# A one-core encoder layer with MoE: one gather over all 512 slots, another split of slot sizes, and where a bias, a scale and a PSUM bank come from

## The chip, the cores and the metric

The kernel runs on one NeuronCore of a Trainium2 chip. The metric is the device time of one execution in microseconds (us), as a median of several. TensorE (PE) multiplies, VectorE (DVE), ScalarE (ACT) and GpSimd (POOL) do the rest of the arithmetic, and SyncE (SP) issues nearly all loads from HBM, in the order in which they are written.

## What is computed

One layer over 256 tokens of 2048 channels, batch 1. A vector c gives six modulation vectors, `mod = SiLU(c) @ W_ada + b_ada`: shift, scale and gate for the mixer and for the FFN. What the change touches is this skeleton of the reference:

```python
h = rms_norm(x, g_mix) * (1 + sc1) + sh1
x = x + g1 * (token_mixer(h, w_in, ...) @ w_out)
h = rms_norm(x, g_ffn) * (1 + sc2) + sh2
x = x + g2 * moe_ffn(h)        # 16 experts, every token goes to two of them
# moe_ffn: for each expert e, its rows xb of h (512 rows in all):
#   hid = silu(xb @ w_gate[e]) * (xb @ w_up[e]);   y = hid @ w_down[e]
```

Everything is float32. With the reference's own inputs the router sends 77, 70, 62, 59, 56, 33, 30, 27, 26, 16, 15, 14, 12, 11, 4 and 0 rows to the experts, sorted by load.

## The kernel before

The program is written in the order in which each engine runs it; engines meet only at semaphores.

**Mixer (0 to about 355 us).** `h` is made in five chunks of channels (`make_h`): for each 128 channels, a matmul of `xa` (x, tokens on the partitions) with `diag`, a diagonal matrix of 1/rms, transposes and scales x at once into a PSUM bank (L409); DVE applies the modulation and `split` writes a hi and a lo part in fp32r. Weights of w_in are split the same way, hi by ACT (L175), lo by DVE or POOL (L176), and three matmuls (`mm3`: hi*hi, lo*hi, hi*lo) make one product of nearly float32 accuracy. `pm()` deals three PSUM banks in turn. Tiles of w_ada run between the pieces: `ada_parts` multiplies on PE into one of two banks `accs`, each with a matmul for the bias at its end (L270); `sum_parts` does it on DVE.

**w_out (about 355 to 470 us).** Four column blocks n, each with two pm banks and 16 weight pieces; `x1_block` on DVE, POOL and ACT adds the result to xa. DVE also sums w_ada for g1 here. Tiles of w_ada for g2 start in block 3 and go on through the routing.

**Routing (470 to 532 us).** Router logits give a 0/1 matrix M (L1001). PE, in its queue after g2 tiles, counts and ranks (L1007 to L1012, into `pp`); DVE sorts the experts by load (`key`, `irow`, `pos`) and builds `oneh` (L1085 to L1087): for each of 512 slots a one in the row of the token that fills it, times its 1/rms. `gather` multiplies xa by oneh in plain float32, first for slots 0 to 255 into pm banks, then, just ahead of the experts, for slots 256 to 511 (L1343), and writes `XT`, the experts' input. `irow` holds the experts' numbers; SP needs it before it can load an expert.

**Experts (532 to 1440 us).** `CAPS` gives the slots per rank: the three busiest get 128, six get 64, six get 32, the last none. `ORDER` mixes the ranks in time. An expert is 12 tiles of 2 MB (8 for gate and up, 4 for down) through a ring of six wide buffers (`wide`): four from the earlier ring, and two (`ringl`) that are laid where the mixer's tiles were. For 128 slots the weights are split and every product is three matmuls; for 64 and 32 it is one plain float32 matmul on a part of the array. An expert whose rows exceed its slots gets a pass of 128 slots in a loop at the end (L1362), which runs as often as a count computed on the chip.

Of the kernel before, what the change touches and what calls it, by code (L numbers as in the profile page):

```python
# [43 lines left out]
CAPS = [128] * 3 + [64] * 6 + [32] * 6 + [0]  # L44
# [72 lines left out]
def body(tc, x_d, prm_d, bg_d, wada_d, win_d, wout_d, egu_d, ed_d, out_d):  # L117
# [107 lines left out]
    psM, s_psM = pool("psM", 3, space=PSUM)  # L225
# [7 lines left out]
    lgp = lgp[:, 0:256]  # L233
    def pm():
        return psM.tile([128, 512], F32, name="pm")
# [19 lines left out]
    def ada_parts(sec, k0, nk, after, acc, bias=None):  # L255
# [4 lines left out]
        def one(g):  # L260
# [139 lines left out]

    def make_h(q):
# [291 lines left out]
    mod2.extend((f, None) for f in steps(ada_parts(2, 0, 4, lambda P: g1_first.append(P), 1, 0)))  # L693
# [18 lines left out]
    for q in range(last):  # L712
# [93 lines left out]
    rt, s_rt = pool("rt")  # L806

# [14 lines left out]
    G.iota(ec, pattern=[[1, 1]], base=0, channel_multiplier=1, allow_small_or_imprecise_dtypes=True)  # L822
    revc = rtile([16, 1], "revc")
# [4 lines left out]
    o = 0  # L828
# [73 lines left out]
    def g1_steps(n):  # L902
        r4s.append(grow())
        if n == 0:
            S.copy(r4s[0], g1_first[0])
# [3 lines left out]
        return steps(sum_parts(2, 4 * n, 4, lambda a: None, n % 2, ENG(G1[n]), lambda: r4s[n], n))  # L909
# [10 lines left out]

    r2, g2p, g1s = [], deque(), {}
# [37 lines left out]

    B3 = [128, 2, 16]  # L960
# [10 lines left out]
    V.reciprocal(sc, sc)  # L971
    sl = rtile(B3, "sl")
# [68 lines left out]
    V.tensor_copy(irow[:, 0:16], po[0:1, 0:16])  # L1041
    order = rtile([128, 16], "order")
# [15 lines left out]
    s_py.close()  # L1058
    s_hp.close()
    s_pb.close()  # L1060
    s_c1.close()
    pg2, s_pg2 = pool("pg2", 1, side="right")
    g2w = pg2.tile([128, D], F32, name="g2w")
    wides += [pg2.tile([128, 2 * RINGW], F32, name=f"ringl{i}") for i in range(RING_LAST)]
    old = wides[:RING + RING_MORE]
    used = [max(i for i, x in enumerate(ring_tiles) if x is a or x is b) for a, b in halves_of]
    wide_ring = deque(wides[RING + RING_MORE:] + [t for _, t in sorted(zip(used, old), key=lambda x: x[0])])

    def wide():
        wide_ring.rotate(-1)  # L1070
        return wide_ring[-1]

    XT = pg2.tile([128, KD, 512], F32, name="XT")

# [350 lines left out]
```

## Time and profile before

| | us |
|---|---|
| median of 3 runs (lowest to highest) | 1436.28 (1435.34 to 1439.57) |
| the profiled execution's own time | 1442.07 |
| its span in the trace | 1440.2 |
| busy: PE / DVE / ACT / POOL | 1247.2 / 693.2 / 417.1 / 160.5 |
| read from HBM | 535.85 MB |

A busy PE is not one at its peak: a matmul's row lasts from its start to its modelled end, and rows overlap. The stretches are best read by two things, the GB/s of the loads and what PE waits for. Times in the rows are us from the start of the span.

### The profile page before, as it was taken

The numbers are of one execution on the slowest core, as the hardware profiler recorded it, in microseconds if no ns is written. First come the engines' busy times: TensorE is split into PE (matmuls) and PEld (weight loads), VectorE is DVE, ScalarE is ACT, GpSimd is POOL, SyncE is SP. The second block draws the span as 40 slices with busy tenths as digits, with TensorE's granted clock in tenths as the row PEclk, the third lists the DMA queues.
The fourth block names the chain that finished last, engine by engine and source line by source line (L and its number), as shares of the span: only waits on it lengthen the run. The fifth ranks groups of instructions, "written<-read, shape, count | busy, mean of one in ns | idle before, by whom it ended". The sixth has DMA issues, their size and how long they took to land.

```text
span 1440.2 us, 17629 instructions
## 1 busy us (share of the span) xinstructions
PE 1247.2 (87%) x6844; PEld 683.4 (47%) x6844; DVE 693.2 (48%) x1271; ACT 417.1 (29%) x754; POOL 160.5 (11%) x127
## 2 busy tenths in 40 slices
PE   5998999998999896999969999689997889858876
PEld 3665776664776372764326743257533222222221
DVE  4466675755795643893228842269611211202112
ACT  4532334445343140771006820048300000000000
POOL 1333332312443000000000000000000000000000
PEclk9999999999999898999989999899999999989988
DMA  9979696889888579998999989999899999999997
GB/s 391 377 312 348 237 375 227 313 334 352 355 301 344 212 296 428 427 415 339 427 426 426 424 315 428 428 425 427 308 420 426 425 427 427 426 427 426 427 427 296
DMA packets 49209, 539.15 MB, mean 374 GB/s; under 512 B 5464, under 2 KB 5592, under 8 KB 7008
## 3 DMA queue, kind: packets, MB, share of 16 engines
q1 hardware_dynamic: 47664, 534.79, 90.7%
q10 hardware_dynamic: 1456, 3.17, 0.6%
q8 instruction: 55, 0.90, 0.3%
q14 instruction: 34, 0.28, 0.1%
HBM read 535.85 MB, written 2.10 MB: 374 GB/s over the span
## 4 chain that ended last, share of the span: by engine, by line
PE 59%; DMA 26%; DVE 7%; issue 3%; ACT 2%; POOL 1%; SPq 0%; DVEq 0%; ACTq 0%; POOLq 0%
PE lbank L171 29%; PE pm L171 18%; DMA ring<-in_e_down_dram 11%; DMA ringl<-in_e_gu_dram 7%; DMA ring<-in_e_gu_dram 7%; PE bank L171 6%; PE ada L171 4%; PE pt L171 1%; DVE ada L294 1%; DMA ring<-in_w_ada_dram 1%; DVE whl L176 1%; DVE el L176 1%; ACT whl L175 1%; DVE z L451 1%; POOL whl L176 0%
## 5 line engine op out<-in xcount | busy, mean ns | idle before, releaser
L171 PE MATMUL pm<-whl,hT 128*128 128x512 f32 x1120 | 296.6, 400 | 9.7 <-DVE whl L176 3.9
L171 PEld LDWEIGHTS pm<-whl,hT 128*128 128x128 f32 x1120 | 208.8, 190 | 82.9 <-issue 12.8
L171 PE MATMUL lbank<-ringl,xr 128*32 128x256 f32 (+1 forms) x1152 | 143.1, 494 | 38.1 <-DMA ringl<-in_e_gu_dram 37.8
L171 PE MATMUL lbank<-el,xs 128*128 128x512 f32 x576 | 138.3, 398 | 9.5 <-ACT el L175 6.5
L176 POOL TENSOR_TENSOR whl<-ring,whl 128x512 fp32r<-128x512 f32 x86 | 120.0, 1407 | 225.4 <-ACT whl L175 201.9
L171 PE MATMUL lbank<-ring,xr 128*32 128x256 f32 (+1 forms) x864 | 104.3, 484 | 34.8 <-DMA ring<-in_e_gu_dram 34.7
L171 PEld LDWEIGHTS lbank<-el,xs 128*128 128x128 f32 x576 | 108.1, 190 | 39.9 <-ACT el L175 9.7
L175 ACT CAST whl<-ring 128x512 fp32r<-128x512 f32 x172 | 99.9, 622 | 72.6 <-PE pm L171 62.5
L171 PE MATMUL bank<-y,gt 128*128 128x512 f32 x240 | 118.0, 614 | 0.0
L1304 DVE TENSOR_TENSOR xa<-xa,bank 128x512 f32<-128x512 f32 x120 | 82.5, 688 | 68.5 <-PE bank L171 68.5
L171 PE MATMUL lbank<-ring,hidT 128*64 128x512 f32 (+1 forms) x576 | 104.6, 630 | 10.9 <-DMA ring<-in_e_down_dram 10.9
L171 PEld LDWEIGHTS lbank<-ringl,xr 128*32 128x32 f32 (+1 forms) x1152 | 52.0, 127 | 129.1 <-issue 68.0
L1295 DVE TENSOR_TENSOR y<-lbank,g2w 128x512 f32<-128x512 f32 x60 | 41.5, 692 | 147.9 <-PE lbank L171 147.9
L176 DVE TENSOR_TENSOR whl<-ring,whl 128x512 fp32r<-128x512 f32 x86 | 83.9, 991 | 38.0 <-ACT whl L175 37.7
L175 ACT CAST el<-ring 128x512 fp32r<-128x512 f32 x144 | 90.0, 625 | 29.3 <-PE lbank L171 21.6
L176 DVE TENSOR_TENSOR el<-ring,el 128x512 fp32r<-128x512 f32 x144 | 92.7, 689 | 0.0
L1191 ACT COPY gt<-bank 128x256 f32<-128x256 f32 x15 | 5.6, 373 | 290.0 <-PE bank L1189 290.0
L1245 DVE TENSOR_TENSOR hid<-hid,lbank 128x512 f32<-128x512 f32 x12 | 8.3, 688 | 164.7 <-PE lbank L171 164.5
L171 PEld LDWEIGHTS lbank<-ring,xr 128*32 128x32 f32 (+1 forms) x864 | 39.1, 127 | 98.8 <-DMA ring<-in_e_gu_dram 48.9
L171 PE MATMUL ada<-ring,cact 128*1 128x512 f32 (+1 forms) x568 | 68.6, 585 | 19.7 <-DMA ring<-in_w_ada_dram 14.0
L171 PE MATMUL lbank<-el,hidT 128*128 128x512 f32 x288 | 74.9, 412 | 12.1 <-DVE el L176 8.3
L175 ACT CAST el<-ringl 128x512 fp32r<-128x512 f32 x96 | 58.7, 624 | 79.5 <-DMA ringl<-in_e_gu_dram 64.8
(377 smaller groups left out, 1185.4 us busy)
## 6 DMA issues: line engine op xcount, KB each, us to landing
ringl<-in_e_gu_dram SPq DMA_DIRECT2D x60, 2048.0 KB, 20.1
ring<-in_e_gu_dram SPq DMA_DIRECT2D x45, 2048.0 KB, 24.3
ring<-in_e_down_dram SPq DMA_DIRECT2D x45, 2048.0 KB, 25.7
ring<-in_w_ada_dram SPq DMA_DIRECT2D x79, 1024.0 KB, 7.1
ring<-in_w_in_dram SPq DMA_DIRECT2D x30, 1024.0 KB, 8.2
ringm<-in_e_gu_dram SPq DMA_DIRECT2D x15, 2048.0 KB, 21.0
ringm<-in_e_down_dram SPq DMA_DIRECT2D x15, 2048.0 KB, 21.5
ring<-in_w_out_dram SPq DMA_DIRECT2D x12, 1024.0 KB, 8.2
```

The costliest lines, as they stand in the source:

```text
L171: E.matmul(out, lhsT=lhsT, rhs=rhs, start=start, stop=stop, skip_group_check=True)
L175: S.copy(hi, src)
L176: (eng or V).tensor_tensor(lo, src, hi.bitcast(F32), op=OP.subtract)
L294: eng.scalar_tensor_tensor(P, w[:, j, :], ck, P, op0=OP.mult, op1=OP.add)
L451: V.tensor_tensor(dst, dst, P[h], op=OP.add)
L1191: S.copy(gt, p[:, :256])
L1245: V.tensor_tensor(hid[:, o], hid[:, o], P[2 * b + 1], op=OP.mult)
L1295: V.tensor_tensor(y, P, g2w[:, c0:c0 + 512], op=OP.mult)
L1304: V.tensor_tensor(a, a, p, op=OP.add)
```

## The change

- `CAPS` becomes two ranks of 128, seven of 64, six of 32.
- The three pm banks are now fixed tiles in a deque; when the last product with `accs[1]` is done (g1's first part), `accs[1]` joins them as a fourth. All w_ada products behind it use `accs[0]`.
- `ada_parts` loses its bias matmul. The rows of the bias come by eight small DMAs on ACT's queue into `bgr`, and `gate_row` adds one row on DVE behind ACT's copy. (The parts that DVE sums keep their bias.)
- `scaled` (ACT) writes x times 1/rms for a chunk into `xn`; `make_h` transposes it with the identity; `diag` is gone.
- The gather is one pass: `x_hi` (ACT) and `x_lo` (DVE) split x times 1/rms into fp32r, `oneh` holds plain ones, and each 128 channels take four fp32r matmuls of 512 columns; ACT writes all of XT. The second gather is gone.
- To make room, the mixer's pools close before the routing (`ones` and `stri` are copied), `xhl` and `oneh` lie where `ringl` was, and `ringl` follows them. The experts' ring now begins with the four older buffers.

```diff
-CAPS = [128] * 3 + [64] * 6 + [32] * 6 + [0]
+CAPS = [128] * 2 + [64] * 7 + [32] * 6 + [0]
...
+    pbanks = deque(psM.tile([128, 512], F32, name=f"pm{i}") for i in range(3))
     def pm():
-        return psM.tile([128, 512], F32, name="pm")
+        pbanks.rotate(-1)
+        return pbanks[-1]
...
-                if g == ng - 1 and bias is not None:
-                    mm(P[0:1, :], ident[0:8, bias:bias + 1], bgt, start=False)
...
+    def scaled(q):
+        k0, nk = CHUNKS[q]
+        for h in range(2):
+            S.activation(xn[:, h, :128 * nk], xa[:, h, 128 * k0:128 * k0 + 128 * nk], AF.Identity, scale=rsx[:, h:h + 1])
...
-                mm(p[:, 128 * h:128 * h + 128], xa[:, h, 128 * k:128 * k + 128], diag[:, h, :])
+                E.transpose(p[:, 128 * h:128 * h + 128], xn[:, h, 128 * c:128 * c + 128], ident)
...
+    def gate_row(sec, q, out, P):
+        S.copy(out, P)
+        o = slice(32 * q, 32 * q + 1)
+        V.tensor_tensor(out[o, :], out[o, :], bgr[o, sec // 3, :], op=OP.add)
...
+    for q in range(4):
+        for a in range(2):
+            nc.scalar.dma_start(bgr[32 * q:32 * q + 1, a, :], bg_d[a:a + 1, 512 * q:512 * q + 512])
...
+    g1_load(1)
+    pbanks.append(accs[1])
...
+    def x_hi():
+        for c, h in parts:
+            o = slice(1024 * c, 1024 * c + 1024)
+            S.activation(xhl[:, 0, h, o], xa[:, h, o], AF.Identity, scale=rs1[:, h:h + 1])
+
+    def x_lo(n):
+        for _ in range(n):
+            c, h = parts.pop(0)
+            o = slice(1024 * c, 1024 * c + 1024)
+            V.scalar_tensor_tensor(xhl[:, 1, h, o], xa[:, h, o], rs1[:, h:h + 1], xhl[:, 0, h, o].bitcast(F32),
+                                   op0=OP.mult, op1=OP.subtract)
...
     V.reciprocal(sc, sc)
+    x_hi()
...
-    mm(pp[:, 16:32], ones, M[:, 0, :], start=False)
+    mm(pp[:, 16:32], one2, M[:, 0, :], start=False)
+    x_lo(2)
...
     V.tensor_copy(irow[:, 0:16], po[0:1, 0:16])
+    x_lo(2)
...
-        V.tensor_scalar(oneh[:, h, :], io512, sl2[:, 0, h:h + 1], rs1[:, h:h + 1], op0=OP.is_equal, op1=OP.mult)
-        V.tensor_scalar(oht, io512, sl2[:, 1, h:h + 1], rs1[:, h:h + 1], op0=OP.is_equal, op1=OP.mult)
-        V.tensor_tensor(oneh[:, h, :], oneh[:, h, :], oht, op=OP.add)
+        V.tensor_scalar(oneh[:, h, :], io512, sl2[:, 0, h:h + 1], None, op0=OP.is_equal)
+        V.scalar_tensor_tensor(oneh[:, h, :], io512, sl2[:, 1, h:h + 1], oneh[:, h, :].bitcast(F32),
+                               op0=OP.is_equal, op1=OP.add)
...
+            for i in range(2):
+                mm(p, xhl[:, i, h, 128 * k:128 * k + 128], oneh[:, h, :], h + i == 0, h + i == 2)
+        S.activation(XT[:, k, :], p, AF.Identity, scale=mod[:, 3, k:k + 1], bias=mod[:, 2, k:k + 1])
...
+    s_phl.close()
+    pl, s_pl = pool("pl", 1, side="right")
+    wides += [pl.tile([128, 2 * RINGW], F32, name=f"ringl{i}") for i in range(RING_LAST)]
...
-    for k in range(KD):
-        gather(1, k, bank)
```

DVE in the routing, from M (which expert each token takes) to the copy of the ranks, `pos`. Before:

```order
L1001 TENSOR_TENSOR M<-oh_3680,oh_3687 128x32
L1029 SCALAR_TENSOR_TENSOR key<-pt_119,rev 128x16
L1030 SCALAR_TENSOR_TENSOR keyc<-pt_119,revc 16x1
L1032 TENSOR_SCALAR rkc<-key,keyc 16x16
L1033 TENSOR_REDUCE rkc<-rkc 16x1
L1035 TENSOR_SCALAR ohc<-ioE,rkc 16x16
L1041 CAST irow<-pt_120 1x16
L1043 COPY order<-pt_120 128x16
L1045 COPY pos<-pt_119 128x48
```

After, in the same place on DVE (`grow_3328` to `grow_3330` are the g2 rows of chunks 1 to 3, `xhl` is written by x_lo):

```order
L1050 TENSOR_TENSOR M<-oh_3608,oh_3615 128x32
L797 TENSOR_TENSOR grow_3328<-grow_3328,bgr 1x512
L797 TENSOR_TENSOR grow_3329<-grow_3329,bgr 1x512
L1004 SCALAR_TENSOR_TENSOR xhl<-xa,rs_3530,xhl 128x1024 x2
L1079 SCALAR_TENSOR_TENSOR key<-pt_122,rev 128x16
...
L1085 TENSOR_SCALAR ohc<-ioE,rkc 16x16
L797 TENSOR_TENSOR grow_3330<-grow_3330,bgr 1x512
L1091 CAST irow<-pt_123 1x16
L1004 SCALAR_TENSOR_TENSOR xhl<-xa,rs_3530,xhl 128x1024 x2
L1094 COPY order<-pt_123 128x16
L1096 COPY pos<-pt_122 128x48
```

Two row additions and two halves of x_lo now stand ahead of `key`, one addition ahead of `irow`, and two more halves of x_lo ahead of `order` and `pos`.

ACT in the same stretch, before, from the router's exponential to the first gather's writes:

```order
L346 ACTIVATE rs_3620<-rs_3620 128x2
L969 ACTIVATE sc<-sc 128x32
L789 COPY grow_3416<-ada_114 128x512
L789 COPY grow_3417<-ada_113 128x512
L789 COPY grow_3418<-ada_114 128x512
L1096 ACTIVATE XT<-pm,mod 128x256 x16
```

After:

```order
L346 ACTIVATE rs_3530<-rs_3530 128x2
L1017 ACTIVATE sc<-sc 128x32
L998 ACTIVATE xhl<-xa,rs_3530 128x1024 x4
L795 COPY grow_3328<-ada_113 128x512
L795 COPY grow_3329<-ada_113 128x512
L795 COPY grow_3330<-ada_113 128x512
L1127 ACTIVATE XT<-pm_120,mod 128x512
```

The four halves of x_hi stand ahead of the copy of g2's chunk 1, and all three copies now read the one bank ada_113 (`accs[0]`), where before they took turns with ada_114.

## Rows read from the trace of the kernel before

**Rows 1.** The page: GB/s in 40 equal slices of the span (36 us each)

```profile
GB/s 391 377 312 348 237 375 227 313 334 352 355 301 344 212 296 428 427 415 339 427 426 426 424 315 428 428 425 427 308 420 426 425 427 427 426 427 426 427 427 296
```

**Rows 2.** Windows (busy us of PE, PEld, DVE, ACT, POOL; clock; DMA share; GB/s)

```profile
1010.00:1050.00 40.00, 37.96 (x152) 20.51 (x154) 22.09 (x37) 12.88 (x21) 0.00 (x0) 1.00 0.83 317
1100.00:1400.00 300.00, 233.39 (x1342) 78.02 (x1346) 53.22 (x100) 4.43 (x10) 0.00 (x0) 0.94 1.01 427
```

**Rows 3.** The page's costliest groups: matmuls of the three 128-slot experts

```profile
L171 PE MATMUL lbank<-el,xs 128*128 128x512 f32 x576 | 138.3, 398 | 9.5 <-ACT el L175 6.5
...
L171 PE MATMUL lbank<-el,hidT 128*128 128x512 f32 x288 | 74.9, 412 | 12.1 <-DVE el L176 8.3
```

**Rows 4.** Timeline of the routing, 478 to 496 us (start us, us, engine, line, operation)

```profile
478.76 0.23 ACT L969 ACTIVATE sc<-sc 128x32 f32<-128x32 f32 x1 [2.25 <-DVE sc L968]
...
482.35 3.59 PE L171 MATMUL ada<-ring,cact 128*1 128x512 f32 x16
482.45 0.59 ACT L789 COPY grow<-ada 128x512 f32<-128x512 f32 x1 [3.46 <-PE ada L171]
...
487.85 1.01 PE L171 MATMUL ada<-bgt,ident 8*1 8x512 f32 x2
488.79 0.62 PE L171 MATMUL pt<-M,ones 128*128 128x16 f32 x4
...
490.40 0.17 DVE L1029 SCALAR_TENSOR_TENSOR key<-pt,rev 128x16 f32<-128x16 f32 x1 [5.61 <-PE pt L171]
...
491.71 3.61 PE L171 MATMUL ada<-ring,cact 128*1 128x512 f32 x32
491.99 0.18 DVE L1045 COPY pos<-pt 128x48 f32<-128x48 f32 x1
...
495.70 0.54 DVE L1085 TENSOR_SCALAR ring<-io,sl,rs 128x512 f32<-128x512 f32 x1
```

**Rows 5.** The chain that ended last: an early w_in piece, then both gathers

```profile
67.58 5.68 PE pm L171 x24
...
499.12 18.77 PE pm L171 x70
517.89 14.31 PE bank L171 x64
```

**Rows 6.** First expert loads on SP's queue, and a window of the second gather

```profile
496.39 0.89 SPq L1312 DMA_DIRECT2D ringl<-in_e_gu_dram  x2
...
524.00:532.00 8.00, 8.00 (x37) 6.05 (x36) 2.72 (x5) 2.27 (x4) 0.00 (x0) 1.00 0.00 2
```

**Rows 7.** Waits of 345 to 478 us (total, times, longest), and a bias matmul

```profile
PE pm L171 <- DVE xg L855: 3.7, 3, 1.8
...
462.84 1.01 PE L171 MATMUL ada<-bgt,ident 8*1 8x512 f32 x2
```

**Rows 8.** Start of the w_out stage, and ACT's own DMAs (issue ns, landing us)

```profile
360.92 2.96 DVE L176 TENSOR_TENSOR whl<-ring,whl 128x512 fp32r<-128x512 f32 x3
...
L1273 ACTq DMA_DIRECT2D out_dram<-xa x8: 338/338/353, 1423.1 to 1434.1; - x8
...
DMA to landing us min/median/max: 2.7/3.1/5.2
```

**Rows 9.** Operations on ACT and DVE by shape (count | busy us, mean ns)

```profile
L375 ACT ACTIVATE hT<-xa 128x2048 fp32r<-128x2048 f32 x2 | 3.8, 1902 | 0.3 <-DMA xa<-in_x_dram 0.3
...
L175 ACT CAST whl<-ring 128x512 fp32r<-128x512 f32 x42 | 24.2, 621 | 18.1 <-PE pm L171 18.1
...
L294 DVE SCALAR_TENSOR_TENSOR ada<-ring,cact,ada 128x512 f32<-128x512 f32 x33 | 24.9, 754 | 1.0
```

**Rows 10.** Transposes by matmul, the DVE step behind one, and a window

```profile
L171 PE MATMUL pt<-diag,xa x60: 274/275/487, 21.6 to 228.0; 128*128 128x128 f32 x60
...
226.98 0.54 DVE L411 TENSOR_SCALAR hf<-pt,mod 128x256 f32<-128x256 f32 x1
...
220.00:240.00 20.00, 18.52 (x100) 12.74 (x101) 12.33 (x25) 7.82 (x15) 6.01 (x4) 1.00 0.34 124
```

More of the change, by code (lines that the diff above doesn't have):

```diff
@@ L266, in run @@
                     k, t = r * g + j, j % 4
-                    mm(P[32 * t:32 * t + 1, :128 * nk], cact[:, k:k + 1], w[:, j, :], start=k < 4,
-                       stop=k >= KD - 4 and (t > 0 or bias is None))
-                if g == ng - 1 and bias is not None:
-                    mm(P[0:1, :], ident[0:8, bias:bias + 1], bgt, start=False)
+                    mm(P[32 * t:32 * t + 1, :128 * nk], cact[:, k:k + 1], w[:, j, :], start=k < 4, stop=k >= KD - 4)
                 if g == ng - 1:
@@ L516, in body @@
         f()
+    scaled(0)
     flush()
@@ L692, in body @@
     g1_first = []
-    mod2.extend((f, None) for f in steps(ada_parts(2, 0, 4, lambda P: g1_first.append(P), 1, 0)))
+    mod2.extend((f, None) for f in steps(ada_parts(2, 0, 4, lambda P: g1_first.append(P), 1)))
     for i in range(4, 33, 4):
@@ L720, in body @@
                 piece(q, PIECES[i])
+            if i == 1:
+                then(lambda q=q: scaled(q + 1))
             for c in PLAN[q][i]:
@@ L822, in body @@
     G.iota(ec, pattern=[[1, 1]], base=0, channel_multiplier=1, allow_small_or_imprecise_dtypes=True)
+    one2 = rtile([128, 128], "one2")
+    V.tensor_copy(one2, ones)
+    stri2 = rtile([128, 128], "stri2")
+    V.tensor_copy(stri2, stri)
     revc = rtile([16, 1], "revc")
@@ L904, in g1_steps @@
         if n == 0:
-            S.copy(r4s[0], g1_first[0])
+            gate_row(2, 0, r4s[0], g1_first[0])
             return []
@@ L957, in body @@
     logit_b(3)
+    s_py.close()
+    s_hp.close()
+    s_pb.close()
+    s_c1.close()
+    pg2, s_pg2 = pool("pg2", 1, side="right")
+    g2w = pg2.tile([128, D], F32, name="g2w")
+    XT = pg2.tile([128, KD, 512], F32, name="XT")
+    phl, s_phl = pool("phl", 1, side="right")
+    xhl = phl.tile([128, 2, 2, D], F32R, name="xhl")
+    oneh = phl.tile([128, 2, 512], F32R, name="oneh")
+    parts = [(c, h) for c in range(2) for h in range(2)]
+    def x_hi():
[8 more added lines that the diff above has]
+                                   op0=OP.mult, op1=OP.subtract)
     B3 = [128, 2, 16]
@@ L1055, in body @@
     pick(start, tmp, cnt)
[L1058 to L1073, printed above, removed]
-    oneh = wide_ring[-1][:, :1024].rearrange("p (h s) -> p h s", h=2)
     sl1 = rtile(B3, "sl1")
@@ L1105, in body @@
     for k in range(KD):
-        gather(0, k, pm)
+        gather(k)
     cntR = rtile([128, 16], "cntR")
@@ L1161, in body, with wide @@
         S.copy(g2w[:, 512 * b:512 * b + 512], p)
+    s_phl.close()
+    pl, s_pl = pool("pl", 1, side="right")
+    wides += [pl.tile([128, 2 * RINGW], F32, name=f"ringl{i}") for i in range(RING_LAST)]
+    old = wides[:RING + RING_MORE]
+    used = [max(i for i, x in enumerate(ring_tiles) if x is a or x is b) for a, b in halves_of]
+    wide_ring = deque([t for _, t in sorted(zip(used, old), key=lambda x: x[0])] + wides[RING + RING_MORE:])
+    def wide():
+        wide_ring.rotate(-1)
+        return wide_ring[-1]
     s_rt.close()
```

37 lines of the change are left out of this document (15 added, 22 removed).

## The prediction

> **What bounds the kernel now.** I read the page's slices first, then windows where they dip, then the timeline of the routing, and last waits and single operations. The slices [rows 1] split the span in two. From slice 15 (540 us) on, the loads run at 424 to 428 GB/s but for three dips (slices 17 and 18, 23, 28) and the end; over 1100 to 1400 us it is 427 GB/s at a DMA share of 1.01, while PE is busy 233 of 300 us [rows 2]. So the experts are bound by their loads: a tile of 2.097 MB takes 4.91 us, and 180 tiles are needed. The dips lie in the three 128-slot experts, the only ones that split their weights; there PE is the bound and the ring is full. Before slice 13 the loads run mostly well under 427 GB/s: the mixer and w_out are bound by PE, with DVE close behind it in w_out. Between the two lies the routing, a chain of small DVE and PE steps and then the gathers, and in it the loads stand still: 2 GB/s in 524 to 532 us [rows 6], because the five free ring buffers are full and the experts have not begun.
>
> The end is therefore set by three things: when PE reaches the routing, when the loads run freely again, and how long they are held up later.
>
> **The change part by part.** The sum is made against the profiled execution's 1442.07 us, which is 5.8 us above the median of 1436.28; I take the same difference off both.
>
> 1. *The third 128-slot expert becomes a 64-slot one.* Its dip, 1010 to 1050 us, ran at 317 GB/s [rows 2]: 40 x (1 - 317/427) = 10.3 us of loading lost. Nothing in 1100 to 1400 us, where only 64 and 32 slots run, shows such a loss, so PE is late nowhere there and the whole of it should come back: **-10.3** (bounds -10.5 and -8). What is late next is the loads themselves.
>
> 2. *The gather and its chain.* Both gathers together run from 499.12 to 532.2 us, the second one alone 14.3 us for 64 instructions [rows 5]. The new gather is 64 fp32r instructions of 512 columns; such instructions run at 5.68/24 = 0.237 us each [rows 5], so 15.2 us. Saving 14 us of PE time is the easy part. The chain ahead of it grows, as the order of DVE and ACT shows:
>  - x_hi on ACT: 2048 columns took 1.902 us, 512 took 0.621 [rows 9], so 1024 about 1.05, and four 4.2. They start behind the exponential (478.99) [rows 4] and end near 483.2; only then comes the copy of g2's chunk 1 (0.59), which before ran at 482.45 [rows 4]. As all chunks now share one bank, PE starts chunk 2 near 484.0, where before it started at 482.35, in spite of the bias matmul that is gone. Its 32 instructions took 5.5 us to 487.85 [rows 4]. The counts (`pp`) stand behind them on PE: 489.5 for 488.79.
>  - DVE must then wait for ACT's copy of chunk 2 (done near 490.2), add a row of 512 (a DVE operation on 512 columns takes 0.754 [rows 9]; I take 0.7) and do two halves of x_lo. One is 1024 columns: between 0.754 and 1.51 (two of 512); I take 1.2. So `key` comes at 493.3, before at 490.40 [rows 4].
>  - `ohc` and its matmul come 1.4 us later, at 494.7. In before `irow` and `pos` followed at once, beside 32 instructions for chunk 3 (3.61 us) [rows 4]. Now DVE's addition for chunk 3 stands ahead of `irow`, so DVE waits for those: 3.6 us at the pace of rows 4, 6.9 if PE is as slow as at 482.35 (16 in 3.59); I take 4.5. With copy and addition that is 500.6; two more halves of x_lo: `pos` is done near 503.4, against 492.2: **11.2 us later**.
>  - From there `oneh` began 3.5 us later [rows 4], now near 506.9; four operations instead of six, 2.4 us: 509.3.
>  - The gather: 62 x 0.237 = 14.7, and some 1.6 us for a start at a low clock (the first gather's 62 last instructions took about 15.2 us, ahead of the g2w matmuls, at 0.224 each they would take 13.9). It ends near **525.6**, where the second gather ended at 532.2: 6.6 us earlier.
>  The loads: in before five tiles lay ready at 532.2 and the sixth could go; now four buffers can be filled early and the two `ringl` wait for the gather's end. One tile of 4.91 us fewer is ready 6.6 us earlier: **-1.7**. When the first tile is issued (496.39 [rows 6], now perhaps 501) no longer matters, since four take 20 us and are there before the gather ends. Bounds: x_lo at 0.75 each, PE at full pace and an x_hi that hides would bring 7 us more; all slow, and with a colder gather, 6 us less: -8 to +5.
>
> 3. *Fourth bank in w_out.* PE waited there for DVE to empty a bank, 3.7 us in three waits [rows 7]; with four banks the next block starts at once. DVE is busy nearly all the time there, so some of it may come back as a wait for split weights. I take **-2.5** (0 to -3.7).
>
> 4. *Bias matmuls.* A pair holds PE for about 0.95 us (487.85 to 488.79) [rows 4]. Those of g2's chunks 1 to 3 are in part 2, g1's lies beside ACT and DVE work. Chunk 0's, inside PE-bound w_out, counts: **-0.95**.
>
> 5. *Transposes of scaled x.* 16 times, four instructions (two float32 matmuls make 64; 60 of them read as 275 ns, mostly latency [rows 10]) become two. But a chunk's modulation on DVE, 0.54 us each [rows 10], and the hi and lo behind it set the pace, five times. I take 0.2 us per chunk of the five: **-1.0** (0 to -3). The scaling by ACT is ten operations of 256 or 512 columns, hidden, since ACT has a piece's time to spare; with no cover it would be under 6 us.
>
> 6. *Eight small DMAs on ACT's queue at the start of w_out.* Each costs ACT some 0.34 us of issue (eight stores took 338 to 353 ns) and lands 2.7 to 5.2 us later [rows 8]. They stand ahead of the first weight splits, and DVE's first row addition waits for them, ahead of its first lo part, which began at 360.92 [rows 8] and which PE waited for. Issue of eight (2.7 us) and the last one's landing make 5.4 to 7.9 us behind ACT's last mixer step; part of it is covered by DVE's own set-up steps ahead of 360.92, the addition (0.7) is not. **+1.5** (0.7 to 4). The Trainium skill, "DMA: Bandwidth & Descriptors", section "Anatomy of one DMA", gives a small DMA about 2.0 us in all; no row here has one so small, and by it this term would be near +0.7.
>
> Sum: -10.3 - 1.7 - 2.5 - 0.95 - 1.0 + 1.5 = **-15 us**: 1427 for the profiled execution, **1421 us** for the median.
>
> **The rivals.**
>
> *A. The gather's gain arrives whole.* If the row additions and x_lo cost the chain nothing, the loads start near 493.5 and never stop: by 533.2 eight tiles have come instead of five, 15 us instead of 1.7; with the other terms 1436.3 - 28 = 1408 us. Against it: DVE's order shows the additions ahead of `key` and `irow`, and ACT's copies behind x_hi.
>
> *B. The routing gets slower than it was.* x_lo at 1.5, chunk 3 at the slow pace: the loads resume later by the +5 of part 2: 1436.3 - 8.3 = 1428 us. For it: PE idles longer ahead of chunk 3 and of the gather.
>
> *C. The dip only moves.* If the third dip's 10.3 us are given back (the loads held up elsewhere, by PE at a low clock between tiles), only parts 2 to 6 stay: 1431.6 us. Against it: 1100 to 1400 us.
>
> *D. The transposes let PE's clock fall.* In 220 to 240 us, which holds a `make_h` with its transposes, of both kinds, the granted clock is 1.00 (2.4 GHz) [rows 10]. A fall like that at 482.35 (16 instructions in 3.59 us, where 32 took 3.61 [rows 4]) would cost about 1.7 us, five times: 1421 + 8 = 1429 us. The Trainium skill, "TensorE: Matmul & The Clock Gate", section "PE-mode transpose", says that PE in transpose mode does not count as busy for the clock gate; by that rule this rival would be likelier, and the window speaks against it.
>
> *E. Overflow, and slower than before.* The third rank now holds 64 rows. From 65 on, its rest takes a pass of 128 slots in the loop at the end, with nothing beside it: matmuls of (138.3 + 74.9)/3 = 71 us [rows 3], so 1421 + 71 = 1492 us. The reference's routing gives that rank 62 rows, two short of it.
>
> **How the numbers follow.** The forecast, 1421, has 0.67; A 0.08; B 0.12; C 0.07; D 0.04; E 0.02. All low bounds together give 1411, all high ones 1436; the range **1411 to 1432** leaves out A's best, E, and the worst of B and C. About 0.3%, 4.3 us, is what a measurement can tell: faster needs less than 1432. The forecast, A, B and D are on that side but for their tails, C is on the border: faster 0.90, same 0.07, slower 0.03.
>
> **What would show it.** Right: no dip in the third of the three old places, 427 GB/s from the second dip to the end; DVE waiting for ACT's copies ahead of `key` and `irow`; the gather ending near 525 us, about 3 us less with the mixer's gain; a stop of the loads of some 5 us ahead of `ringl`; no wait of PE for a bank in w_out. Wrong: a third dip in another place (part 1); a gather that ends ahead of 518 or behind 532 us (part 2); PE waiting for `whl` instead of a bank (part 3); the first w_out product more than 3 us late (part 6); any pass of the last loop (E).

## The result, and the profile after

The changed kernel takes 1429.73 us (median of five executions, 1423.43 to 1430.22), the kernel before 1439.26 us beside it (1435.34 to 1439.57): a ratio of 0.9927 (95% interval 0.9909 to 0.9944), or 10.5 us faster. The forecast was 15 us. Run once more later (e5 below), the ratio was 0.9920 (0.9898 to 0.9942). Of the 8.7 us between the forecast's 1421 and 1429.73, some 4.5 are a gain that fell short; most of the rest is the kernel before, whose median went up from 1436.28 to 1439.26 with two more executions.

The two profiles must be read with care: that of before (1442.07 us) lies at the upper end of its kernel's times, that of after (1423.43) is the lowest of its five. They differ by 18.6 us, the kernels by 10.5.

The page of after, GB/s in 40 slices of 35.5 us, answers to [rows 1]:

```profile
GB/s 391 355 349 317 248 349 228 322 342 354 366 293 379 176 355 428 426 427 334 427 426 427 427 331 429 426 427 427 426 427 426 427 427 427 426 426 427 427 427 291
```

Two dips are left where before had three. Windows around the three old places (busy us of PE, PEld, DVE, ACT, POOL; clock; DMA share; GB/s), first of before, then of after:

```profile
620.00:690.00 70.00, 65.00 (x274) 34.57 (x272) 35.83 (x61) 25.78 (x43) 0.00 (x0) 1.00 0.92 376
800.00:880.00 80.00, 73.91 (x308) 41.03 (x308) 42.69 (x74) 30.53 (x51) 0.00 (x0) 0.98 0.93 376
980.00:1080.00 100.00, 93.91 (x398) 51.73 (x397) 55.53 (x93) 39.37 (x65) 0.00 (x0) 1.00 0.93 382
```

```profile
620.00:690.00 70.00, 64.23 (x270) 31.99 (x272) 32.69 (x60) 21.28 (x36) 0.00 (x0) 1.00 0.94 381
800.00:880.00 80.00, 73.77 (x311) 37.14 (x311) 38.56 (x69) 24.72 (x42) 0.00 (x0) 1.00 0.94 385
980.00:1080.00 100.00, 85.51 (x456) 28.69 (x456) 19.50 (x34) 1.34 (x3) 0.00 (x0) 0.98 1.01 426
```

Loading lost, window x (1 - GB/s / 427): 8.4, 9.6 and 10.5 us before; 7.5, 7.9 and 0.2 after.

The routing of after answers to [rows 4 to 6] (start us, us, engine, line, operation, and in brackets the idle time before it and what ended it):

```profile
474.68 4.25 ACT L998 ACTIVATE xhl<-xa,rs 128x1024 fp32r<-128x1024 f32 x4
...
478.84 0.56 ACT L795 COPY grow<-ada 128x512 f32<-128x512 f32 x1
...
479.45 3.19 PE L171 MATMUL ada<-ring,cact 128*1 128x512 f32 x16 [3.00 <-ACT grow L795]
...
480.38 0.19 DVE L1050 TENSOR_TENSOR M<-oh,oh 128x32 f32<-128x32 f32 x1
...
482.46 1.89 PE L171 MATMUL ada<-ringm,cact 128*1 128x512 f32 x16
...
485.05 0.68 DVE L797 TENSOR_TENSOR grow<-grow,bgr 1x512 f32<-1x512 f32 x1 [3.77 <-ACT grow L795]
...
485.75 2.48 DVE L1004 SCALAR_TENSOR_TENSOR xhl<-xa,rs,xhl 128x1024 fp32r<-128x1024 f32 x2
...
489.66 4.92 PE L171 MATMUL ada<-ring,cact 128*1 128x512 f32 x32
...
495.27 0.69 DVE L797 TENSOR_TENSOR grow<-grow,bgr 1x512 f32<-1x512 f32 x1 [6.20 <-ACT grow L795]
495.99 0.16 DVE L1091 CAST irow<-pt 1x16 int32<-1x16 f32 x1
496.19 2.48 DVE L1004 SCALAR_TENSOR_TENSOR xhl<-xa,rs,xhl 128x1024 fp32r<-128x1024 f32 x2
...
498.67 0.20 DVE L1096 COPY pos<-pt 128x48 f32<-128x48 f32 x1
...
503.80 5.73 PE L171 MATMUL pm<-oneh,xhl 128*128 128x512 f32 x12 [9.22 <-DVE oneh L1118]
...
521.45 0.87 SPq L1352 DMA_DIRECT2D ringl<-in_e_gu_dram  x2
```

All four waits that the forecast named stand there: PE for the copy behind x_hi (3.00 us), DVE for the copies of chunks 2 and 3 (3.77 and 6.20 us), and PE for the one-hot (9.22 us). I measure the routing from `M`, DVE's last step ahead of the counts, to the issue that ends the standstill of the loads: 484.60 to 532.22 us before, **47.6 us**; 480.38 to 521.45 after, **41.1 us**. But before had five tiles ready there and after four, and a tile is 4.91 us of loading. And 47.6 us is a slow routing of the old kind: e1, with the same code up to the experts, took 42.6. Both ends in before:

```profile
484.60 0.19 DVE L1001 TENSOR_TENSOR M<-oh,oh 128x32 f32<-128x32 f32 x1
...
532.22 0.33 SPq L1312 DMA_DIRECT2D ring<-in_e_gu_dram  x1
```

### The profile page after: what moved, and what is told of

Read it like the earlier page. It is cut to its first block, busy times and chain, and to the rows that moved or that the text cites. A ratio compares the mean times of both kernels' runs of the same rounds, so it can differ in the third digit from the quotient of the medians.

```text
span 1421.7 us, 17020 instructions
## 1 busy us (share of the span) xinstructions
PE 1202.6 (85%) x6638; PEld 625.6 (44%) x6638; DVE 628.1 (44%) x1168; ACT 363.7 (26%) x661; POOL 161.1 (11%) x127
## 3 DMA queue, kind: packets, MB, share of 16 engines
q10 hardware_dynamic: 1472, 3.19, 0.6%
## 4 chain that ended last, share of the span: by engine, by line
PE 33%; DMA 33%; DVE 2%; ACT 1%; issue 1%; DVEq 0%; ACTq 0%
PE lbank L171 24%; DMA ring<-in_e_down_dram 14%; DMA ring<-in_e_gu_dram 9%; DMA ringm<-in_e_gu_dram 6%; PE bank L171 4%; PE pm L171 3%; PE ada L171 2%; DMA ringl<-in_e_down_dram 2%; DMA ringl<-in_e_gu_dram 2%; DVE el L176 0%; DVE xhl L1004 0%; ACT xhl L998 0%; ACT el L175 0%; PE pt L171 0%; PE pt L892 0%
## 5 line engine op out<-in xcount | busy, mean ns | idle before, releaser
L171 PE MATMUL lbank<-ring,xr 128*32 128x256 f32 (+1 forms) x1216 | 155.4, 494 | 41.3 <-DMA ring<-in_e_gu_dram 41.3
L171 PEld LDWEIGHTS lbank<-ring,xr 128*32 128x32 f32 (+1 forms) x1216 | 55.2, 127 | 133.6 <-issue 63.4
L171 PE MATMUL lbank<-ring,hidT 128*64 128x512 f32 (+1 forms) x416 | 81.7, 683 | 30.8 <-DVE hidT L1303 15.8
L171 PE MATMUL lbank<-ringl,xr 128*32 128x256 f32 (+1 forms) x608 | 80.3, 511 | 31.9 <-DMA ringl<-in_e_gu_dram 31.9
L171 PE MATMUL lbank<-el,xs 128*128 128x512 f32 x384 | 91.2, 395 | 7.3 <-ACT el L175 5.5
L171 PE MATMUL lbank<-ringm,xr 128*32 128x256 f32 (+1 forms) x608 | 78.4, 494 | 21.6 <-DMA ringm<-in_e_gu_dram 20.9
L171 PE MATMUL ada<-ring,cact 128*1 128x512 f32 (+1 forms) x568 | 70.4, 599 | 21.7 <-DMA ring<-in_w_ada_dram 13.1
L171 PEld LDWEIGHTS lbank<-el,xs 128*128 128x128 f32 x384 | 71.3, 188 | 27.4 <-ACT el L175 7.6
L171 PE MATMUL lbank<-ringl,hidT 128*64 128x512 f32 (+1 forms) x416 | 74.2, 598 | 4.7 <-DMA ringl<-in_e_down_dram 4.7
L171 PEld LDWEIGHTS bank<-y,gt 128*128 128x128 f32 x240 | 42.1, 193 | 73.3 <-issue 70.9
L454 DVE TENSOR_TENSOR z<-z,pm 128x512 f32<-128x512 f32 x72 | 48.5, 685 | 57.5 <-PE pm L171 57.5
```

The costliest lines, as they stand in the source:

```text
L171: E.matmul(out, lhsT=lhsT, rhs=rhs, start=start, stop=stop, skip_group_check=True)
L454: V.tensor_tensor(dst, dst, P[h], op=OP.add)
```

## The experiments

All are timed in five rounds beside the kernel before. "Mended" stands for the kernel of e4. Ratios are to the kernel before, with 95% intervals.

**e1: the slots alone.** The kernel before with one line of the change:

```
-CAPS = [128] * 3 + [64] * 6 + [32] * 6 + [0]
+CAPS = [128] * 2 + [64] * 7 + [32] * 6 + [0]
```

> The kernel before with the new slot sizes alone (two of 128, seven of 64). My theory: the third dip's 10.3 us of lost loading come back whole, so 10 us less than the kernel before (ratio 0.993), no dip between 1000 and 1060 us, and everything ahead of the experts as before. The rival that the dip only moves: 0 to 3 us less, and a new stretch under 400 GB/s elsewhere. If the whole change's 9.5 us in the median are the slots alone, then the other parts together bring nothing in the median, though the two profiles show 6 us ahead of the experts.

Measured: 1429.87 us for 1437.04, ratio 0.9950 (0.9934 to 0.9967), so 7.2 us (4.7 to 9.5). The third dip is gone in its windows:

```profile
980.00:1080.00 100.00, 87.87 (x444) 29.25 (x442) 21.67 (x40) 1.94 (x4) 0.00 (x0) 0.98 1.01 426
```

The window says 10.3 us, the times say 7.2. The code ahead of the experts is that of before, and yet the two profiles differ there: e1 reached `M` 2.7 us later (487.32) and ended the standstill 2.3 us earlier. `key` waits for PE in both (2.33 us here, 5.61 in [rows 4]), and the sixteen matmuls that took 3.59 us in before, at a granted clock of 0.50, took 1.90 here, at 1.00:

```profile
483.74 1.90 PE L171 MATMUL ada<-ring,cact 128*1 128x512 f32 x16
...
529.95 0.33 SPq L1312 DMA_DIRECT2D ring<-in_e_gu_dram  x1
```

So executions of one code differ by some microseconds ahead of the experts. e12 tries the slots again on a steadier kernel.

**e2: all but the slots.** The changed kernel with the old line of e1 put back:

```
-CAPS = [128] * 2 + [64] * 7 + [32] * 6 + [0]
+CAPS = [128] * 3 + [64] * 6 + [32] * 6 + [0]
```

> The changed kernel with the old slot sizes (three of 128). My theory: the loads resume 11 us earlier with one tile fewer ready, 5 to 6 us less than the kernel before (ratio 0.996), and the three dips are back at some 8, 9 and 10 us. The rival that the parts ahead of the experts bring nothing outside the one profile: 0 us, ratio 1.000, with the gather's end near where the kernel before has it.

Measured: 1435.72 us for 1437.04, ratio 0.9986 (0.9967 to 1.0005) over twelve executions that reach from 1428.35 to 1440.56. So all the rest of the change, five parts, is worth 1 or 2 us, not 5. Something in it costs about what the rest brings; e3 to e8 look for it.

**e3: the matmul back in `make_h`.** The changed kernel with the diagonal matmul for scaling and transposes:

```
-                E.transpose(p[:, 128 * h:128 * h + 128], xn[:, h, 128 * c:128 * c + 128], ident)
+                mm(p[:, 128 * h:128 * h + 128], xa[:, h, 128 * k:128 * k + 128], diag[:, h, :])
```

> The changed kernel with the transposes of x undone: make_h multiplies x with the diagonal matrix again and ACT scales nothing. In the changed kernel's profile the mixer ended 2.3 us later than before, behind stretches at a granted clock of 0.59, 0.72 and 0.76 after make_h. If the transposes let PE's clock fall (the rival), those stretches are back at 1.00, the mixer ends 2 to 4 us earlier than in the changed kernel and the time is 2 to 4 us less (1426). If the falls are chance, the same or up to 1 us more than the changed kernel (1430), and the falls are there as often.

Measured: 1427.05 us, ratio 0.9921 (0.9901 to 0.9942), no different from the changed kernel's 0.9927 and 0.9920. In its profile the mixer was quicker (`M` at 477.76 us for 480.38), but the routing took 43.9 us for 41.1 and gave it back; why, e5 shows.

**e4: the chain mended.** The changed kernel with three moves: the row additions of g2 are issued behind the one-hot, all of x_lo right behind `M`, and chunk 2 of g2 gets the second accumulator, so that PE need not wait for ScalarE's copy behind x_hi:

```
-        V.tensor_tensor(out[o, :], out[o, :], bgr[o, sec // 3, :], op=OP.add)
+
+        def add():
+            V.tensor_tensor(out[o, :], out[o, :], bgr[o, sec // 3, :], op=OP.add)
+        add() if sec == 2 else row_adds.append(add)
...
-        return sec, 4 * q, 4, lambda P: gate_row(sec, q, out, P), 0
+        return sec, 4 * q, 4, lambda P: gate_row(sec, q, out, P), 1 if sec == 5 and q == 2 else 0
...
+    x_lo(4)
     g2_run(len(g2p) - NG2)
...
-    x_lo(2)
...
-    x_lo(2)
...
+    for add in row_adds:
+        add()
```

> The changed kernel with the routing's chain mended: the g2 row additions stand behind oneh on DVE instead of ahead of key and irow, all four halves of x_lo stand right behind M where DVE waits for PE anyhow, and g2's chunk 2 uses the other bank, so that PE does not wait for ACT's copy behind x_hi. My theory (the chain, not the gather, ate the gain): the gather ends 10 to 13 us earlier against M than in the changed kernel (where it ends 41 us after M), the ringl loads start as much earlier, and the time is 10 to 13 us less, about 1418. The rival that PE's gather or the loads themselves set the restart: less than 4 us less.

Measured: **1411.84 us** (1410.36 to 1413.94), ratio 0.9826 (0.9808 to 0.9843): 25 us under the kernel before and, by the ratios, 13 to 15 under the changed one, more than expected. Timeline of its routing:

```profile
480.54 0.19 DVE L1055 TENSOR_TENSOR M<-oh,oh 128x32 f32<-128x32 f32 x1
480.65 4.86 DVE L1009 SCALAR_TENSOR_TENSOR xhl<-xa,rs,xhl 128x1024 fp32r<-128x1024 f32 x4
...
485.43 0.17 DVE L1084 SCALAR_TENSOR_TENSOR key<-pt,rev 128x16 f32<-128x16 f32 x1
...
487.23 0.18 DVE L1100 COPY pos<-pt 128x48 f32<-128x48 f32 x1
...
493.38 3.02 PE L171 MATMUL pm<-oneh,xhl 128*128 128x512 f32 x12
...
508.31 0.87 SPq L1359 DMA_DIRECT2D ringl<-in_e_gu_dram  x2
```

`M` stands where it stood, `pos` comes 11.4 us earlier, and the loads run 13.1 us earlier: `M` to loads is 27.8 us. Against the old routing (42.6 us in e1, 47.6 in before) the single-pass gather was worth 15 to 20 us less a tile all along; the additions and x_lo in DVE's order, and chunk 2's wait for the bank, hid it.

**e5: the changed kernel again**, unaltered, for a second profile.

> The changed kernel once more, unaltered. Its profile of 1423.43 us was the fastest of its five executions (median 1429.73), and the granted clock there was 0.959, against 0.948 to 0.952 in the three slowest. Theory: the gap between the profile and the median is TensorE's clock, in the routing and the first half of the gather (0.53 at 500 to 510 us in the profile) and in the two remaining dips (loads lost: 7.5 and 7.8 us there, 9.8 and 9.9 with the diagonal matmul back). Then a profile with a clock near 0.952 shows dips of some 10 us each and a time of 1428 to 1430. Rival: the gap lies ahead of the routing, in the mixer or w_out; then the dips stay at 7.5 and 7.8 us and the routing begins some 4 us or more later than at 480.4.

Measured: 1426.93 us (1424.12 to 1431.86) for 1439.22, ratio 0.9920 (0.9898 to 0.9942); this time the profiled execution was the slowest, 1431.86, at a granted clock of 0.949 for 0.959. PE in the routing, then the issue that ends the standstill:

```profile
480.40 3.59 PE L171 MATMUL ada<-ring,cact 128*1 128x512 f32 x16 [2.90 <-ACT grow L795]
483.77 3.18 PE L171 MATMUL ada<-ringm,cact 128*1 128x512 f32 x16
...
492.25 5.74 PE L171 MATMUL ada<-ring,cact 128*1 128x512 f32 x32
...
507.22 5.73 PE L171 MATMUL pm<-oneh,xhl 128*128 128x512 f32 x12 [9.23 <-DVE oneh L1118]
...
525.29 0.87 SPq L1352 DMA_DIRECT2D ringl<-in_e_gu_dram  x2
```

The second sixteen matmuls of chunk 2 took 1.89 us in the first profile, at a granted clock of 1.00, and 3.18 here, at 0.59. `M` is 0.9 later (481.32), `M` to loads is 44.0 us for 41.1, and the two dips lose 9.5 and 9.6 us for 7.5 and 7.9. That is 7.5 of the 8.3 us between the two spans, in the places that the theory named; the rival (all of it ahead of the routing) falls. Half of the theory fell with it: in the dips the granted clock is 1.00 and 0.98, as before, so what made them deeper isn't the clock there, and it stays open. In the routing it is the clock. A routing in which PE waits has a length that differs between executions, since PE's g2 matmuls stand in DVE's chain and run at either level.

**e6: the additions alone.** Of e4's three moves only the first:

```
-        V.tensor_tensor(out[o, :], out[o, :], bgr[o, sec // 3, :], op=OP.add)
...
+        add() if sec == 2 else row_adds.append(add)
...
+    for add in row_adds:
+        add()
```

> The changed kernel with one thing altered: the row additions of g2 on VectorE are issued behind the one-hot of the gather instead of right behind ScalarE's copies. x_lo keeps its place and all four chunks of g2 keep one bank. Theory: the wait of the addition for the copy of chunk 3 (6.20 us idle at 495.27, with the 4.92 us of matmuls behind the counts in front of it) is the larger part of what the mended kernel gained. Then irow follows the count's matmul at once, key comes near 485.8 and pos near 490.4 for 498.67, the gather ends some 8 us earlier, and the time is 8 to 11 us under the changed kernel's (about 1417 to 1420). Rival: x_hi on ScalarE, which makes TensorE wait 3.00 us for the copy of chunk 1, and x_lo behind the counts are the larger part; then pos comes at 494 or later and the time is 5 us under the changed kernel's at most (1423 or more).

Measured: 1416.36 us (1413.03 to 1419.86) for 1439.22, ratio 0.9841 (0.9820 to 0.9861): by the ratios 11 to 12 of e4's 13 to 15 us. Its timeline:

```profile
480.12 0.19 DVE L1055 TENSOR_TENSOR M<-oh,oh 128x32 f32<-128x32 f32 x1
...
480.23 2.47 DVE L1009 SCALAR_TENSOR_TENSOR xhl<-xa,rs,xhl 128x1024 fp32r<-128x1024 f32 x2
...
487.13 0.17 DVE L1084 SCALAR_TENSOR_TENSOR key<-pt,rev 128x16 f32<-128x16 f32 x1 [4.43 <-PE pt L171]
...
488.67 0.16 DVE L1096 CAST irow<-pt 1x16 int32<-1x16 f32 x1 [0.60 <-PE pt L171]
```

`irow` follows the count's matmul at once, where it stood 6.20 us behind a copy of something it doesn't need. What remains is 4.43 us of DVE waiting for the counts behind PE's slow chunk 2, and a pair of x_lo halves (2.5 us) ahead of `pos`. In e4 the counts come earlier and all of x_lo stands in the wait: `pos` follows `M` by 6.7 us there, by 11.1 here. Which of e4's other two moves brought how much wasn't tried. The theory holds.

**e7 and e10, beside e4 and e9: the transposes, on the mended kernel.** e7 and e10 are one kernel, the mended one with e3's matmul; e9 is e4 again, on the same chip as e10 and against the same runs of the kernel before.

> The mended kernel with make_h's diagonal matmul back in place of the scaled rows and transposes. Theory: transposes cost about 2 us of the mixer (with the matmul the third chunk's hf stands at 94.4 us in three profiles of three, with transposes at 96.35, 94.09 and 95.76), and the routing no longer swallows the gain, since nothing in it waits for TensorE's g2 matmuls; then M comes 1 to 3 us earlier than at 480.5 and the time is 1409 to 1411. Rival: the form of the transposes is worth nothing and the fall of the clock after 94 us comes by chance in either kind: 1411 to 1413, as the mended kernel's 1411.84.

> The mended kernel (transposes of scaled rows) once more, to stand beside the version with the diagonal matmul on the same chip and against the same runs of the kernel before; apart, the two had ratios of 0.9826 and 0.9800 with intervals that overlap. Theory: the transposes are worth nothing either way, since the mean of limR over the profiles is 361.5 us with transposes (six) and 360.3 us with the matmul (four), which is inside the spread of either kind; then the two medians lie within 2 us of each other. Rival: they cost 2 to 4 us, through TensorE's clock behind make_h; then this one is that much slower than the other.

> The mended kernel with the diagonal matmul back in make_h, beside the one with transposes. Theory: within 2 us of it. Rival: 2 to 4 us faster than it, with the third chunk's hf near 94.4 us, where the transposes have 95.8 to 97.7.

Measured with the matmul: 1410.83 us, ratio 0.9800 (0.9781 to 0.9820), and again 1410.55, ratio 0.9800 (0.9781 to 0.9819). With transposes: ratio 0.9826 (e4), and again 1412.22 us, 0.9819 (0.9801 to 0.9837). The matmul is ahead both times: where the two ran side by side by 1.7 us in the medians and 2.7 by the ratios, e7 against e4 by 3.7 by the ratios. The intervals overlap, so that by the times alone neither theory is settled.

The profiles say more. Take `hf`, DVE's first step behind a transposed tile, from the first of chunk 1 to the first of chunk 3, here in e7 and in after:

```profile
22.36 0.54 DVE L411 TENSOR_SCALAR hf<-pt,mod 128x256 f32<-128x256 f32 x1
...
94.41 0.55 DVE L411 TENSOR_SCALAR hf<-pt,mod 128x256 f32<-128x256 f32 x1
```

```profile
21.36 0.54 DVE L414 TENSOR_SCALAR hf<-pt,mod 128x256 f32<-128x256 f32 x1
...
96.35 0.54 DVE L414 TENSOR_SCALAR hf<-pt,mod 128x256 f32<-128x256 f32 x1
```

In all five profiles with the matmul (before, e1, e3, e7, e10) this takes 71.9 to 72.1 us. With transposes it takes 71.9 to 72.0 in four of nine (e2, e9, e11, e12), 73.2 in two (e4, e6) and 74.7 to 75.0 in three (after, e5, e8): 1.2 us more on the mean. The granted clock goes with it. In 20 to 30 us, behind the first `make_h`, it is 0.70 to 0.83 in those five and 0.88 to 1.00 in the other nine; in 58 to 68 us, behind the second, it is 0.83 in the three longest and 1.00 in the other eleven. Further on both kinds show falls (at 120 to 130 us 0.82 to 0.90 with the matmul, 0.74 to 0.99 with transposes), and from chunk 3 to chunk 5 they don't differ (133.8 and 133.7 us on the mean). `limR`, among DVE's last steps ahead of w_out, comes at 359.74 us on the mean of e3, e7 and e10 and at 361.15 on that of the nine.

So the sharper rival, that the first `hf` of the third chunk tells them apart, holds in part: with the matmul it came at 93.2 to 94.5 us each time, with transposes at 95.8 to 97.7 in four profiles of nine. What is left to chance is how the falls are spread: five of nine against none of five would come about once in sixteen times without a cause.

**e8: three banks.** The mended kernel without the line that gives w_out its fourth bank:

```
-    pbanks.append(accs[1])
```

> The mended kernel with three banks for w_out, as before the change, for four. It is tried on the mended kernel because its times lie closer together (1410.36 to 1413.94) than the changed kernel's. Theory: the fourth bank is what shortened the w_out stage by 5.9 us (the forecast gave it 2.5 and the lost bias matmul 0.95); then the stage takes 4 to 6 us longer and the time is 1415 to 1418. Rival: the stage is bound by VectorE's and ScalarE's splits of w_out in either case, and the fourth bank only moves waits: 1411 to 1413, and the stage's shortening came from a clock that fell less in it (0.91 for 0.83 at 360 to 380 us).

Measured: 1417.54 us (1413.11 to 1419.16), ratio 0.9851 (0.9828 to 0.9873): 3.6 us behind e4 and 4.6 behind e9 by the ratios, though the intervals of e4 and e8 touch. PE's waits in w_out (total, times, longest), first of e8, which answer to [rows 7], then of after:

```profile
PE pm L171 <- DVE xg L879: 3.6, 3, 1.7
PE pm L171 <- ACT whl L175: 3.2, 1, 3.2
```

```profile
PE pm L171 <- ACT whl L175: 3.4, 2, 3.2
```

The three waits for a bank are there with three banks, gone with four, and nothing has come in their place. From `limR` to `rs` (DVE's start of the stage to the first step behind it) e8 takes 115.4 us, e4 111.9, and no profile with four banks more than 113.1.

**e11: g2 ahead of the counts.** The mended kernel with one number altered; of the chunk behind the order matmul half (16 of 32 matmuls) moved ahead of the counts, not the whole, as the expectation has it:

```
-G2, G2_MID, NG2 = [1, 2, 1, 1], 1, 2
+G2, G2_MID, NG2 = [1, 2, 1, 1], 1, 0
```

> The mended kernel with all of g2's matmuls issued ahead of the counts on TensorE; so far the last chunk stood behind the one-row order matmul and held up the gather (486.94 to 493.45 us, at half the clock, where the one-hot's first half is ready at 492.2). Theory: the counts end by 485.4, when VectorE has made x_lo anyway, so key stays where it is; the gather starts with the one-hot, 1 us earlier, at the higher clock; the loads run again at 506 to 507.5 us for 508.31 and the time is 1 to 2.5 us under the mended kernel's beside it. Rival: ScalarE's copy of chunk 1 behind x_hi (to 480.2 us) and the last w_ada loads push the counts past x_lo, key comes at 487 or later, and the time is the same or 1 to 2 us longer.

Measured: 1411.80 us, ratio 0.9822 (0.9805 to 0.9839), as the mended kernel. PE's timeline:

```profile
484.60 3.59 PE L171 MATMUL ada<-ring,cact 128*1 128x512 f32 x16
490.00 4.74 PE L171 MATMUL pm<-oneh,xhl 128*128 128x512 f32 x12 [1.81 <-DVE oneh L1122]
494.58 1.07 PE L171 MATMUL ada<-oneh,xhl 128*128 128x512 f32 x4
```

The gather did start with the one-hot, 11.8 us behind `M` for 12.8, but its first twelve matmuls took 4.74 us for 3.02, and `M` to loads came out at 28.5 us for 27.8. The expectation fell, through the clock: the sixteen matmuls ahead of the gather ran at a granted 0.50 and its start at 0.63, where in e4 thirty-two matmuls (6.51 us) stand ahead of it and it starts at 1.00.

**e12: three experts of 128 slots**, on the mended kernel:

```
-CAPS = [128] * 2 + [64] * 7 + [32] * 6 + [0]
+CAPS = [128] * 3 + [64] * 6 + [32] * 6 + [0]
```

> The mended kernel with three experts of 128 slots for two, as before the change. The slots alone, on the kernel before, gave 7.2 us (ratio 0.9950, 0.9934 to 0.9967), though the dip that they remove had lost 10.7 us of loading in the profile of before and 0.1 in that run's. Tried on the mended kernel, whose executions lie closer together. Theory: the dip is worth what its window lost, 10 to 11 us, and the 7.2 fell short because the executions differ by some microseconds ahead of the experts; then the time is 1420 to 1423 us and a third dip near 1000 us loses 10 us. Rival: a part of the dip is given back, since the loads have time in hand behind it; then the time is 1417 to 1420 with the same dip in the windows.

Measured: 1420.68 us (1418.49 to 1426.91), ratio 0.9880 (0.9861 to 0.9899): 7.8 and 8.8 us behind e4 and e9 by the ratios. The third dip is back and loses 9.1 us:

```profile
980.00:1080.00 100.00, 92.53 (x490) 43.24 (x488) 40.41 (x70) 21.34 (x36) 0.00 (x0) 0.98 0.95 388
```

That lies between theory and rival, nearer to the first: a dip is worth about what its window lost, and this window lost 9.1 us, not 10.3. A remainder of up to 1.3 us is within the interval of either ratio.

## Why the prediction was right or wrong

The sign and the range held; the size was two thirds of the forecast's. What was said to bound the kernel held in all profiles: span = time at which the loads run freely + loading lost in the dips + a constant. After: 521.45 + 15.6 + 884.6 = 1421.7; e5: 525.29 + 19.1 + 885.6; e4: 508.31 + 16.6 + 884.3; e12: 508.92 + 26.9 + 883.6; the others with four tiles ready have 883 to 886. For before and e1, with one tile more ready, the constant is 879, 5 us less: the ready tile of part 2 (4.91 us) as it was priced.

| part | forecast, us | measured, us | by |
|---|---|---|---|
| 1 slots | -10.3 | -7 to -9 | e1; e12 against e4, e9 |
| 2 gather and chain | -1.7 | -1.6 to +6.3 by the pair of profiles, +2.5 on the mean | `M` to loads, plus a tile |
| 3 fourth bank | -2.5 | -3.6 to -4.6 | e8 against e4, e9 |
| 4 bias matmul | -0.95 | not taken apart | |
| 5 transposes | -1.0 | +1 to +4; `limR` +1.4 | e7, e10 against e4, e9 |
| 6 small DMAs | +1.5 | about -0.4 | start of w_out |

**Part 1, right mechanism, over-sized.** The price was read from one dip in one profile. Dips of the 128-slot experts lost 7.5 to 10.9 us in the profiles, so the third one of before was among the deepest. The bound of -8 was in the text; the value should have been the mean of the three dips (9.5). In e12 the window lost 9.1 and the times say 7.8 and 8.8; in e1 they say 7.2. Rival C falls: nowhere behind 980 us are loads lost in any kernel with two such experts.

**Part 2, right in each wait, mis-sized in the sum.** x_hi took 4.25 us (4.2 forecast), `pos` came 10.9 us later against `M` (11.2), the standstill ended 6.5 us earlier (6.6). A pair of x_lo halves took 2.48 us (2.4), chunk 3 of g2 4.92 (4.5). But all this is set against one profile of before, whose own routing was slow: 47.6 us from `M`, where the same code took 42.6 in e1. The two of the old kind average 45.1 us, the four of the new kind (after 41.1, e2 42.0, e3 43.9, e5 44.0) 42.7; with the tile the part is a loss of 2.5 us, and no gain of 1.7. The step that went wrong is the pace of the g2 matmuls and of the gather's start (its first twelve took 5.73 us for 2.88, where I gave the start 1.6 us): I put the new ones at a middle pace and took those of before as that one profile has them, but in either kernel they run at either level. Rival B's +5 lies inside what the pairs give, and its 1428 us is near the measured time. Rival A had the larger truth in it: take the additions out of the chain and 11 to 12 us appear (e6), with the rest of the mend 13 to 15 (e4). What it was against was right for the kernel as written.

**Part 3, right**, at its far end: the waits were 3.7 us, and all of them came back. My discount for waits on split weights was not called for: PE waits for those at the stage's start in both kernels (3.0 us before, 3.4 after), and no new one came.

**Part 4, open.** With three banks the stage from `limR` to `rs` is still 1.8 us shorter than before (117.2), which holds the bias matmul's 0.95; the rest wasn't traced.

**Part 5, wrong in sign.** PE's busy time did fall: 30 transposes at 273 ns where 60 matmuls took 275 [rows 10]. It brought nothing: where the clock didn't fall, chunk 1 to chunk 3 takes 72.0 us in either kind. And the mixer ends later, by 1.4 us on the mean of `limR`, of which 1.2 lie between chunk 1 and chunk 3. The step that failed is the one that set rival D aside: it took a clock of 1.00 from one window at 220 to 240 us, which holds the last `make_h`, for all five. The falls come behind the first two. The windows behind the second, first of before and then of after:

```profile
60.00:65.00 5.00, 5.00 (x27) 3.25 (x29) 2.12 (x4) 2.29 (x5) 2.58 (x2) 1.00 0.79 328
```

```profile
60.00:65.00 5.00, 5.00 (x20) 3.41 (x19) 1.50 (x3) 1.94 (x4) 2.28 (x2) 0.77 0.79 329
```

D's price for one fall was near: 1.7 us, and the profiles show 1.2 to 1.4 behind the first block and 1.4 to 1.6 behind the second. Its number was not: eight falls behind the first two blocks in nine profiles, where D had five in each. The Trainium skill, "TensorE: Matmul & The Clock Gate", section "PE-mode transpose", says that such transposes don't count as busy for the clock gate; five profiles of nine agree with it behind one block or both, four show no such fall, so here it is a risk and not a rule.

**Part 6, wrong in sign, small.** The eight DMAs did hold ACT's queue, 2.37 us of issue, and its first weight split slipped from 354.86 to 361.87 us. But PE in before had the first pair of matmuls early and then waited 2.97 us for DVE's lo part; now it waits once, 3.19 us, ahead of the first pair, and its third matmul comes 7.1 us behind the mixer's last transposes (356.40 to 363.52) for 7.5 (354.11 to 361.65). The delay took the place of a wait that I had named and not credited. The section of the Trainium skill's "DMA: Bandwidth & Descriptors" that part 6 names, "Anatomy of one DMA", is on the path of DMAs that GpSimd issues, while these eight were issued by ACT; no run here measured their landing. The start of w_out in after:

```profile
358.99 2.37 ACTq L821 DMA_DIRECT2D bgr<-in_bg_dram  x8
...
360.82 0.40 DVE L845 TENSOR_TENSOR triE<-ioE,ioR 128x256 f32<-128x256 f32 x1
...
361.30 0.18 DVE L853 TENSOR_SCALAR limR<-capR 128x16 f32<-128x16 f32 x1
```

DVE's own set-up also got shorter, with POOL not yet at its splits: `triE` took 1.41 us before, `limR` 1.07, beside POOL's first three splits:

```profile
358.31 4.42 POOL L176 TENSOR_TENSOR whl<-ring,whl 128x512 fp32r<-128x512 f32 x3
...
358.44 1.41 DVE L826 TENSOR_TENSOR triE<-ioE,ioR 128x256 f32<-128x256 f32 x1
```

**E** didn't come: the loads run to the end (291 GB/s in the last slice of after), which leaves no place for a pass of 71 us.

In sum, with middle values: -8 for the slots, +2.5 for the chain, -4 for the bank, -0.95 for the bias as priced, +1.4 for the transposes and -0.4 for the start make -9.5 us, and 10.5 and 11.5 were measured; without the slots -1.5, where e2 measured 1 to 2. The forecast came this near in part by luck: slots, chain and transposes were 9 us too good, bank and start 3 us too bad.

## What to carry to other kernels

An in-order engine that carries a latency chain should get no operation with a far-off input in that chain, however cheap it is: three additions of 0.7 us, for rows that are needed only behind the gather, cost 11 to 12 us, because two of them wait (3.77 and 6.20 us) for matmuls and a copy in other queues. When a faster step comes with a longer chain, price the chain with its side work moved away as well; the difference is what a reordering is worth, and here it was larger than the change. And don't price a part by one window or one profile where the clock or the depth differs from place to place: take all windows of the kind, and both levels.

## What the runs showed of the hardware

- PE's pace behind a wait. The same 16 one-row matmuls of 512 columns took 1.89 to 1.90 us at a granted clock of 1.00 (2.4 GHz) and 3.59 at 0.50 (1.2 GHz). The first twelve matmuls of the gather took 5.73 us after PE had idled 9.22 (clock 0.51), 4.74 after sixteen slow matmuls and 1.81 idle (0.63), and 3.02 straight behind thirty-two others (1.00). Removing work ahead of a step can therefore cost as much as it saves (e11).
- The clock behind PE-mode transposes, as told in part 5: 0.70 to 0.83 behind the first or second block in five profiles of nine, at a cost of 1.2 to 3.0 us, and 0.89 to 1.00 there, at no cost, in all five with matmuls that do the same with twice the instructions.
- DVE beside POOL. The same 128x256 comparison took 0.40 us with POOL idle and 1.41 while POOL made its 1.4 us splits, and a 128x16 step 0.18 and 1.07. Within after, one 128x512 lo part took 0.67 us (at 362.62, mostly ahead of POOL's next split) and the next 1.42 beside it.
